# Hybrid encoder layer on Trainium2: the mixer's norm factors by power, attention heads in pairs, probabilities flipped by bank

## The chip, the cores and the metric

The kernel runs on one core of a Trainium2 chip. The metric is the device time of one execution in microseconds (us). Before the change it is 1005.02 us in the median of three runs (1003.6 to 1005.17). The engines are named as in the profile: PE (TensorE, matrix products; PEld its weight loads), DVE (VectorE), ACT (ScalarE), POOL (GpSimd) and SP (SyncE, which issues the loads). SBUF is the memory on the chip; PSUM is the small memory of eight banks into which PE writes, a bank holding 512 float32 numbers in each of 128 partitions.

## What is computed

One layer over 512 tokens of 1024 channels in float32, cut here to its frame:

```python
x = x + 0.5 * swiglu(rmsnorm(x, ffn1_norm), ffn1_w_gate, ffn1_w_up, ffn1_w_down)
proj = rmsnorm(x, mix_norm) @ w_in                     # 1024 -> 3*512 + 256 + 128 + 32
qa, ka = rmsnorm(q part by head, a_q_norm), rmsnorm(k part by head, a_k_norm)
out_a = chunked_relbias_attention(qa, ka, va, a_rel_bias)   # A: 8 heads of 64
out_b = mla_attention(...)                             # B: 8 heads, q and k of 64 + 32, v of 64
x = x + concat(out_a, out_b) @ w_out
x = x + 0.5 * swiglu(rmsnorm(x, ffn2_norm), ffn2_w_gate, ffn2_w_up, ffn2_w_down)
x = rmsnorm(x, final_norm)
```

`rmsnorm` multiplies by `rsqrt(mean(x*x) + EPS)` and a gain. Both attentions are softmax attentions in which a query sees its own chunk of 64 tokens and the chunks before it; A adds a bias by relative position to the scores, B makes q and k from low-rank latents and turns 32 of their columns by a rotary table. Every query and key part is normed (mean over 64, 32, 256 or 128 columns), which needs one factor per token and head.

## The kernel before

The work is staged as feed-forward block 1, mixer, feed-forward block 2. Every matrix product is split into a high and a low part so that three passes give float32 accuracy (`mm3`, lines 153 to 156): each product is three matmuls, on lines 154, 155 and 156. Weights come from HBM in units of 1024 columns (tag "raw", four buffers) and are split by ACT (high) and POOL or DVE (low) into tags "whi" and "wlo" (`wunit`, lines 140 to 151). The order on every engine is worked out by a scheduler when the kernel is built: it goes by the order of the program, shifted forward by 150 instructions where `tc.high_priority(offset=150)` stands, and by when a buffer of a tag comes free; a tile takes a free buffer of its tag when its first write is scheduled.

The mixer (lines 243 to 574) first makes the projections (`in_proj`, lines 310 to 320): the latents, qA, kA and vA, each as eight rank-128 steps into four banks, one for each 128 tokens. `bank` (lines 305 to 308) gives the banks: group 0 is s, s, tr, tr, group 1 is t, t, t, pv. The latents, uq, ukv and the value projection use group 1, qA and kA group 0. From the sums of squares `factors` (lines 272 to 285) makes the norm factors: a multiply and an add on DVE, then `rsqrt` (lines 116 to 123), which is Ln and Exp on ACT (each with a load of its table) and a refining step of four DVE instructions. POOL scales qB and kB and does the rotary turn (`rope`, lines 287 to 300).

Then the 16 heads run through a pipeline (lines 562 to 574), of three steps for each head:
- `front` (lines 464 to 501): PE transposes q and k into a "tr" bank, ACT and DVE copy the high and low part out (`evac`, lines 456 to 458). For A one transpose serves two heads, whose channels are partitions 0 to 63 and 64 to 127; the bias is loaded by SP, negated by DVE and masked by POOL.
- `softmax` (lines 503 to 523): for the query blocks i = 3, 2, 1, 0 PE makes the scores into "s" banks (512, 384, 256 and 256 columns, causal), DVE adds the bias and takes the minimum (line 518), ACT takes the exponential and its sum (line 520), DVE the reciprocal (line 521), POOL multiplies (line 522).
- `flip` and `values` (lines 525 to 559): PE transposes the probabilities, ten blocks of 128 x 128 in the order of the query blocks, into three "t" banks; ACT and DVE copy high and low parts into "whi" and "wlo" buffers; then PE multiplies with the values into the "pv" bank, two heads into one.

After it come `w_out` and the second feed-forward block, whose last norm uses POOL's power on 128 x 2 numbers (line 626).

Of the kernel before, what the change touches and what calls it, by code (L numbers as in the profile page):

```python
# [10 lines left out]
F32 = mybir.dt.float32  # L11
# [6 lines left out]
P = 128  # L18
# [6 lines left out]
NH = 8  # L25
# [14 lines left out]
def tile_macaron_block(  # L40
# [203 lines left out]
    with tc.tile_pool(name="mix", bufs=1, side="left", reuse_waits="tile") as mp:  # L244
# [24 lines left out]
        dve.tensor_scalar(out=nq[:, 0:1], in0=g(C_AQ), scalar1=-(HD ** -0.5), scalar2=None, op0=ALU.mult)  # L269
        dve.tensor_scalar(out=nq[:, 1:2], in0=g(C_BQ), scalar1=-(QK ** -0.5), scalar2=None, op0=ALU.mult)  # L270

        def factors(ss, n, width, scaled, name):

            f = mp.tile([P, NT, n], F32, tag="f_" + name, name="f_" + name)
            y = mp.tile([P, NT, n], F32, tag="y_" + name, name="y_" + name)
            y2 = mp.tile([P, NT, n], F32, tag="z_" + name, name="z_" + name)
            if scaled:
                dve.tensor_tensor(out=f, in0=ss, in1=vtok.unsqueeze(2).broadcast_to([P, NT, n]), op=ALU.mult)
                dve.tensor_scalar(out=f, in0=f, scalar1=1.0 / width, scalar2=EPS, op0=ALU.mult, op1=ALU.add)
            else:  # L280
                dve.tensor_scalar(out=f, in0=ss, scalar1=1.0 / width, scalar2=EPS, op0=ALU.mult, op1=ALU.add)
            rsqrt(f, f, y, y2)
            if scaled:
                dve.tensor_tensor(out=f, in0=f, in1=rtok.unsqueeze(2).broadcast_to([P, NT, n]), op=ALU.mult)
            return f
# [16 lines left out]
        with tc.tile_pool(name="ps2", bufs=1, space=PSUM, reuse_waits="tile") as ps:  # L302
            NB = {"s": 2, "tr": 2, "t": 3, "pv": 1}

            def bank(group, i, name):

                tag = (("s",) * NB["s"] + ("tr",) * NB["tr"], ("t",) * NB["t"] + ("pv",) * NB["pv"])[group][i]
                return ps.tile([P, 512], F32, tag=tag, name=name, bufs=NB[tag])
# [26 lines left out]
            yt = mp.tile([P, NT], F32, tag="yt", name="yt")  # L335
            zt = mp.tile([P, NT], F32, tag="zt", name="zt")
            rsqrt(rtok, vtok, yt, zt)
# [5 lines left out]
            fcq = factors(ssl[:, 0], 1, 256, True, "cq")  # L343
            fkv = factors(ssl[:, 1], 1, 128, True, "ckv")
            fkr = factors(ssl[:, 2], 1, 32, True, "kr")
# [17 lines left out]
            def qk_proj(off, dst, name):  # L363
# [4 lines left out]
                f = factors(ss, NH, HD, True, name)  # L368
# [26 lines left out]
            fn = factors(ssn, NH, HD, False, "qn")  # L395
            fp = factors(ssp, NH, ROPE, False, "qp")
# [27 lines left out]
            fk = factors(ssk, NH, HD, False, "kn")  # L424
# [37 lines left out]
            shared = {}  # L462

            def front(h):

                if h < NH:
                    if h % 2 == 0:
                        pr = h // 2
                        hs = slice(pr * P, (pr + 1) * P)
                        qh, ql, kh, kl = sets[0 if pr == 0 else 1 + (pr - 1) % 2]  # L470
                        evac(qh, ql, transposes(lambda t: qA[:, t, hs]), nq[:, 0:1])
                        evac(kh, kl, transposes(lambda t: kA[:, t, hs]), g(C_AK))
                        shared["A"] = qh, ql, kh, kl
                    r = slice((h % 2) * HD, (h % 2 + 1) * HD)
                    ops = tuple(t[r, :] for t in shared["A"])
                    bias = mp.tile([P, S], F32, tag="bias", name="bias", bufs=2)
                    nc.sync.dma_start(out=bias, in_=bias_tab[h])
                    dve.tensor_scalar(out=bias, in0=bias, scalar1=-1.0, scalar2=None, op0=ALU.mult)
                    pool.memset(bias[0:HD, S - HD:S], BIG)
                    return ops + (bias,)  # L480
                b = h - NH
                if b == 0:
# [8 lines left out]
                    pool.memset(mask[0:HD, S - HD:S], BIG)  # L491
# [9 lines left out]
                return qh[0:QK, :], ql[0:QK, :], kh, kl, mask  # L501

            def softmax(qh, ql, kh, kl, bias):

                pa = wraw.tile([P, 1024], F32, tag="raw", name="pa")
                pb = wraw.tile([P, 1024], F32, tag="raw", name="pb")
                pi = [pb[:, 256:384], pb[:, 0:256], pa[:, 512:896], pa[:, 0:512]]
                mn = small.tile([P, NT], F32, tag="mn", name="mn", bufs=4)
                sm = small.tile([P, NT], F32, tag="sm", name="sm", bufs=4)
                s3 = ps.tile([P, 512], F32, tag="s", name="s3", bufs=NB["s"])  # L510
                s2 = ps.tile([P, 512], F32, tag="s", name="s2", bufs=NB["s"])
                s01 = ps.tile([P, 512], F32, tag="s", name="s01", bufs=NB["s"])
                for i, so in ((3, s3), (2, s2), (1, s01[:, 256:512]), (0, s01[:, 0:256])):
# [11 lines left out]
            def flip(pi):  # L525
# [9 lines left out]
                for i in (3, 2, 1, 0):  # L535
                    for j in range(i + 1):
                        tt, o = where[j]
                        pe.transpose(tt[:, o + i * P:o + (i + 1) * P], pi[i][:, j * P:(j + 1) * P], ident)  # L538
# [189 lines left out]
```

## Time and profile before

| | before |
|---|---|
| median of 3 runs | 1005.02 us (1003.6 to 1005.17) |
| profiled execution | 1005.75 us, its span in the trace 1004.0 us |
| PE busy | 980.4 us (98%), 4579 matmuls |
| DVE, ACT, POOL busy | 397.7, 387.3, 591.5 us (40%, 39%, 59%) |
| chain that ended last | PE 88%, DVE 4%, POOL 2%, DMA 2%, ACT 1% |

The feed-forward blocks fill the first 390 and the last 410 us; the projections of the mixer lie at about 390 to 490 us and the heads at about 480 to 588 us, partly over one another. An engine's busy time counts a matmul to its modelled end, and matmuls overlap: so the distance from one start to the next, not the duration, tells what a matmul costs PE. In a timeline the idle time ahead of an instruction and what ended it stand in brackets. PEclk is the granted clock of PE, 1.00 being the higher of its two levels, 2.4 GHz, and 0.5 the lower, 1.2 GHz.

### The profile page before, as it was taken

Reading aid. Unit: us, or ns where it says so; the run is one execution under the profiler, and the core shown is the slowest. Engines: PE = TensorE matmul, PEld = TensorE weight load, DVE = VectorE, ACT = ScalarE, POOL = GpSimd, SP = SyncE. Lnnn points to the kernel's source line nnn. Section 1 sums busy time; section 2 is a strip of 40 time slices with the busy share of each in tenths; the row PEclk is TensorE's granted clock in tenths of the full one; section 3 lists DMA queues with packets and bytes.
Section 4 is the critical chain, followed back from the end, with each engine's and each line's share of the span. In section 5 each row is a group of like instructions: output and inputs, shape, how many; then the busy total and the mean of one; then the engine's idle time right before and its main releaser. Section 6 shows DMA issues by size and latency. Waiting matters only on the chain.

```text
span 1004.0 us, 12060 instructions
## 1 busy us (share of the span) xinstructions
PE 980.4 (98%) x4579; PEld 813.8 (81%) x4579; DVE 397.7 (40%) x687; ACT 387.3 (39%) x648; POOL 591.5 (59%) x429
## 2 busy tenths in 40 slices
PE   7999999999999999998999999999999999999996
PEld 4888888888888889786778988888888888888886
DVE  7533333432212215677688855243332333200002
ACT  4333233332222225754578853252332323322320
POOL 8586667667555522277345577677657666645540
PEclk8999999999999999999999999999999999999998
DMA  6422222232333334210010053223332322333302
GB/s 204 140 97 101 94 100 88 101 105 79 95 95 99 95 102 127 84 63 1 22 43 1 2 189 105 84 86 103 105 104 85 105 95 90 90 104 95 100 16 84
DMA packets 28714, 89.90 MB, mean 90 GB/s; under 512 B 3440, under 2 KB 5616, under 8 KB 28656
## 3 DMA queue, kind: packets, MB, share of 16 engines
q1 hardware_dynamic: 27504, 88.08, 27.4%
q10 hardware_dynamic: 1152, 1.05, 0.3%
q8 instruction: 36, 0.59, 0.2%
q14 instruction: 22, 0.18, 0.1%
HBM read 87.02 MB, written 2.10 MB: 89 GB/s over the span
## 4 chain that ended last, share of the span: by engine, by line
PE 88%; DVE 4%; POOL 2%; issue 2%; DMA 2%; ACT 1%; SPq 0%; POOLq 0%; DVEq 0%; ACTq 0%
PE gu L155 16%; PE gu L156 16%; PE gu L154 16%; PE dn L156 8%; PE dn L154 8%; PE dn L155 8%; PE pj L156 2%; PE pj L154 2%; PE pj L155 2%; PE wo L154 1%; PE wo L156 1%; PE wo L155 1%; PE t L538 1%; PE s L154 1%; PE tr L453 1%
## 5 line engine op out<-in xcount | busy, mean ns | idle before, releaser
L150 POOL TENSOR_TENSOR wlo<-raw,whi 128x1024 fp32r<-128x1024 f32 x138 | 323.5, 2345 | 152.0 <-ACT whi L149 152.0
L149 ACT CAST whi<-raw 128x1024 fp32r<-128x1024 f32 (+3 forms) x165 | 166.9, 1012 | 456.5 <-PE gu L155 258.0
L155 PE MATMUL gu<-xl,whi 128*128 128x512 f32 x352 | 139.4, 396 | 3.8 <-DVE xl L104 3.6
L154 PE MATMUL gu<-xh,whi 128*128 128x512 f32 x352 | 138.7, 394 | 0.8 <-ACT whi L149 0.8
L156 PE MATMUL gu<-xh,wlo 128*128 128x512 f32 x352 | 138.6, 394 | 0.0
L154 PE MATMUL gu<-x2h,whi 128*128 128x512 f32 x352 | 136.9, 389 | 0.0
L155 PE MATMUL gu<-x2l,whi 128*128 128x512 f32 x352 | 136.8, 389 | 0.0
L156 PE MATMUL gu<-x2h,wlo 128*128 128x512 f32 x352 | 136.8, 389 | 0.0
L169 POOL TENSOR_TENSOR us<-us,gs 128x512 f32<-128x512 f32 x44 | 58.1, 1321 | 108.6 <-DVE us L167 106.8
L168 DVE SCALAR_TENSOR_TENSOR gs<-th,gs 128x512 f32<-128x512 f32 x44 | 90.9, 2069 | 31.8 <-ACT th L166 31.8
L165 DVE TENSOR_TENSOR gs<-gu,rs 128x512 f32<-128x512 f32 x44 | 30.4, 691 | 175.3 <-PE gu L156 163.3
L202 DVE SCALAR_TENSOR_TENSOR x<-dn,x 128x512 f32<-128x512 f32 (+1 forms) x17 | 11.2, 660 | 193.7 <-PE dn L156 193.7
L155 PEld LDWEIGHTS gu<-xl,whi 128*128 128x128 f32 x352 | 66.9, 190 | 21.2 <-DVE xl L104 7.8
L154 PEld LDWEIGHTS gu<-xh,whi 128*128 128x128 f32 x352 | 67.2, 191 | 15.6 <-ACT whi L149 1.6
L156 PEld LDWEIGHTS gu<-xh,wlo 128*128 128x128 f32 x352 | 66.9, 190 | 13.9 <-DVE wlo L150 0.2
L155 PEld LDWEIGHTS gu<-x2l,whi 128*128 128x128 f32 x352 | 66.1, 188 | 13.8
L156 PEld LDWEIGHTS gu<-x2h,wlo 128*128 128x128 f32 x352 | 66.1, 188 | 13.8
L154 PEld LDWEIGHTS gu<-x2h,whi 128*128 128x128 f32 x352 | 66.1, 188 | 13.6
L154 PE MATMUL dn<-h1h,whi 128*128 128x512 f32 x176 | 68.5, 389 | 0.0
L155 PE MATMUL dn<-h1l,whi 128*128 128x512 f32 x176 | 68.5, 389 | 0.0
L156 PE MATMUL dn<-h1h,wlo 128*128 128x512 f32 x176 | 68.5, 389 | 0.0
L167 DVE SCALAR_TENSOR_TENSOR us<-gu,rs 128x512 f32<-128x512 f32 x44 | 30.3, 689 | 65.2 <-PE gu L156 65.2
(318 smaller groups left out, 1826.8 us busy)
## 6 DMA issues: line engine op xcount, KB each, us to landing
raw<-in_gu SPq DMA_DIRECT2D x87, 512.0 KB, 3.6
raw<-in_dn SPq DMA_DIRECT2D x32, 512.0 KB, 3.5
raw<-in_dn SPq DMA_DIRECT2D x16, 384.0 KB, 3.1
raw<-in_w_in SPq DMA_DIRECT2D x12, 512.0 KB, 3.4
raw<-in_w_out SPq DMA_DIRECT2D x8, 512.0 KB, 4.4
x<-in_xT SPq DMA_DIRECT2D x8, 256.0 KB, 5.5
bias<-in_bias_tab SPq DMA_DIRECT2D x8, 256.0 KB, 2.8
raw<-in_w_in SPq DMA_DIRECT2D x4, 416.0 KB, 3.3
```

The costliest lines, as they stand in the source:

```text
L149: act.copy(hi[:, cc], raw[:, cc])
L150: (lo_on or pool).tensor_tensor(out=lo[:, cc], in0=raw[:, cc], in1=hi[:, cc].bitcast(F32), op=ALU.subtract)
L154: pe.matmul(out, lhsT=ah, rhs=bh, start=start, stop=False)
L155: pe.matmul(out, lhsT=ah, rhs=bl, start=False, stop=False)
L156: pe.matmul(out, lhsT=al, rhs=bh, start=False, stop=stop)
L165: dve.tensor_tensor(out=gs, in0=gup[0], in1=rs, op=ALU.mult)
L167: dve.scalar_tensor_tensor(out=us, in0=gup[1], scalar=0.5, in1=rs, op0=ALU.mult, op1=ALU.mult)
L168: dve.scalar_tensor_tensor(out=gs, in0=th, scalar=1.0, in1=gs, op0=ALU.add, op1=ALU.mult)
L169: pool.tensor_tensor(out=us, in0=us, in1=gs, op=ALU.mult)
L202: dve.scalar_tensor_tensor(out=x[dt][:, h], in0=pt[:, h], scalar=0.5, in1=x[dt][:, h], op0=ALU.mult, op1=ALU.add)
L453: pe.transpose(pt[0:src(t).shape[1], t * P:(t + 1) * P], src(t), ident)
L538: pe.transpose(tt[:, o + i * P:o + (i + 1) * P], pi[i][:, j * P:(j + 1) * P], ident)
```

## The change

Four things are changed, all in the mixer.
- `factors` and `rtok` use one POOL instruction that raises to the power -0.5, in place of Ln, Exp and the refining step; several norms go through one call (the three of the latents; the two of qB).
- The banks: "s" has four (was two), "tr" one (was two), "t" two (was three). Group 0 is s four times, group 1 is t, t, tr, pv.
- A's heads go through `front` and `softmax` in pairs. For each query block the score matmuls of the two heads are issued in turn, each head on its half of the rows. The bias is no longer negated: the queries keep their sign and the DVE instruction scales by -1. The second head's bias sits in the tag "wc"; the probabilities of i = 1 sit in halves of `rs` and `ssum`, the others in one "raw" buffer instead of two.
- One reciprocal over all four query blocks of a head, after its last exponential, and then POOL's four products. `flip` goes bank by bank (keys 3 and 2, keys 1, keys 0), each copied out as soon as it is full.

```diff
-        def factors(ss, n, width, scaled, name):
...
+        mhalf = mp.tile([P, 2 * NT * NH], F32, tag="mhalf", name="mhalf")
+        pool.memset(mhalf, -0.5)
+        def factors(parts, n, scaled, name):
+            f = mp.tile([P, len(parts), NT, n], F32, tag="f_" + name, name="f_" + name)
+            for i, (ss, width) in enumerate(parts):
...
+                dve.tensor_scalar(out=f[:, i], in0=src, scalar1=1.0 / width, scalar2=EPS, op0=ALU.mult, op1=ALU.add)
+            flat = f.rearrange("p i t n -> p (i t n)")
+            pool.tensor_tensor(out=flat, in0=flat, in1=mhalf[:, 0:len(parts) * NT * n], op=ALU.pow)
...
-            NB = {"s": 2, "tr": 2, "t": 3, "pv": 1}
+            NB = {"s": 4, "tr": 1, "t": 2, "pv": 1}
...
-                tag = (("s",) * NB["s"] + ("tr",) * NB["tr"], ("t",) * NB["t"] + ("pv",) * NB["pv"])[group][i]
+                tag = (("s",) * 4, ("t", "t", "tr", "pv"))[group][i]
...
-            rsqrt(rtok, vtok, yt, zt)
+            pool.tensor_tensor(out=rtok, in0=vtok, in1=mhalf[:, 0:NT], op=ALU.pow)
...
-            fcq = factors(ssl[:, 0], 1, 256, True, "cq")
-            fkv = factors(ssl[:, 1], 1, 128, True, "ckv")
-            fkr = factors(ssl[:, 2], 1, 32, True, "kr")
+            fcq, fkv, fkr = factors([(ssl[:, 0], 256), (ssl[:, 1], 128), (ssl[:, 2], 32)], 1, True, "lat")
...
+            def front_a(pr):
...
+                evac(qh, ql, transposes(lambda t: qA[:, t, hs]), nq[:, 0:1])
+                evac(kh, kl, transposes(lambda t: kA[:, t, hs]), g(C_AK))
+                for e in range(2):
+                    bias = (mp.tile([P, S], F32, tag="bias", name="bias", bufs=2) if e == 0
+                            else work.tile([P, S], F32, tag="wc", name="bias"))
+                    nc.sync.dma_start(out=bias, in_=bias_tab[2 * pr + e])
+                    pool.memset(bias[0:HD, S - HD:S], -BIG)
...
+            def softmax(heads):
...
+                for i in (3, 2, 1, 0):
...
+                        bk = [ps.tile([P, 512], F32, tag="s", name=f"s{i}", bufs=NB["s"]) for _ in heads]
...
+                    for j, (a, b) in enumerate(((0, 2), (0, 3), (1, 2))):
+                        for o, hd in zip(so, heads):
+                            pe.matmul(o, lhsT=hd[a][:, ii], rhs=hd[b][:, 0:nn], start=j == 0, stop=j == 2)
+                    for o, hd, (pi, mn, sm) in zip(so, heads, out):
+                        dve.tensor_tensor_reduce(out=pi[i], in0=o[:, 0:n], in1=hd[4][:, S - n:S], op0=ALU.add, op1=ALU.min,
+                                                 scale=-1.0, scalar=3e38, accum_out=mn[:, i:i + 1])
+                        act.activation(pi[i], pi[i], AF.Exp, bias=mn[:, i:i + 1], scale=-1.0, accum_out=sm[:, i:i + 1])
+                for pi, mn, sm in out:
+                    dve.reciprocal(sm, sm)
+                    for i in (3, 2, 1, 0):
+                        pool.tensor_tensor(out=pi[i], in0=pi[i], in1=sm[:, i:i + 1].broadcast_to([P, (i + 1) * P]), op=ALU.mult)
...
+                for keys, copies in ((((3, 0), (2, -256)), (...)), (((1, -128),), (...)), (((0, 0),), (...))):
+                    tt = ps.tile([P, 512], F32, tag="t", name="tp", bufs=NB["t"])
+                    for j, o in keys:
+                        for i in range(NT - 1, j - 1, -1):
+                            pe.transpose(tt[:, o + i * P:o + (i + 1) * P], pi[i][:, j * P:(j + 1) * P], ident)
+                    for h_, l_, c0, c1 in copies:
+                        act.copy(h_, tt[:, c0:c1])
+                        dve.tensor_tensor(out=l_, in0=tt[:, c0:c1], in1=h_.bitcast(F32), op=ALU.subtract)
...
+            fronts = [lambda pr=pr: front_a(pr) for pr in range(4)] + [lambda b=b: front_b(b) for b in range(NH)]
...
             for it in range(-2, n + 1):
+                pis = prob.pop(it, [None])
+                for e, pi in enumerate(pis):
...
+                        cur = head, flip(pi)
...
+                    if e == 0:
+                        with (tc.high_priority(offset=150) if it < 1 else ExitStack()):
+                            if 0 <= it + 1 < n:
+                                prob[it + 1] = softmax(qk.pop(it + 1))
+                            if it + 2 < n:
+                                qk[it + 2] = fronts[it + 2]()
+                    if last:
+                        values(*last)
+                    last = cur
```

## Rows read from the trace of the kernel before

**Rows 1.** windows: stretch, length, busy of PE, PEld, DVE, ACT, POOL; PEclk, DMA, GB/s

```profile
469.90:474.13 4.23, 0.00 (x1) 0.03 (x1) 2.98 (x9) 1.03 (x2) 0.51 (x3) 1.00 0.00 0
474.13:490.00 15.87, 15.87 (x71) 12.25 (x71) 6.72 (x16) 6.13 (x14) 1.87 (x2) 0.89 0.00 0
490.00:580.00 90.00, 88.60 (x573) 74.31 (x573) 77.93 (x277) 71.78 (x209) 48.29 (x97) 1.00 0.07 19
541.00:588.50 47.50, 46.82 (x318) 42.22 (x317) 39.38 (x137) 40.02 (x111) 26.10 (x47) 1.00 0.13 45
```

**Rows 2.** timeline of PE: start, us, line, out<-in, shapes, count [idle before]

```profile
474.13 1.09 PE L453 MATMUL tr<-ident,qA 128*128 128x128 f32 x4 [4.25 <-DVE kA L371]
...
477.56 0.39 PE L154 MATMUL pj<-whi,xh 128*128 128x512 f32 x1
477.79 0.39 PE L155 MATMUL pj<-wlo,xh 128*128 128x512 f32 x1
...
489.98 0.50 PE L156 MATMUL pj<-whi,xl 128*128 128x512 f32 x1
...
498.26 0.48 PE L154 MATMUL pv<-PAh,VAh 128*128 128x512 f32 x1
```

**Rows 3.** timeline of PE where two heads' scores meet (x2: merged)

```profile
501.62 0.28 PE L156 MATMUL pv<-PBh,VAl 128*128 128x256 f32 x1
501.83 0.49 PE L154 MATMUL s<-xh,xh 64*128 64x512 f32 x2
...
502.72 0.33 PE L538 MATMUL t<-ident,pb 128*128 128x128 f32 x1
```

**Rows 4.** timeline of PE, end of one head's scores

```profile
504.51 0.28 PE L155 MATMUL s<-xl,xh 64*128 64x256 f32 x1
504.62 0.28 PE L156 MATMUL s<-xh,xl 64*128 64x256 f32 x1
504.83 0.33 PE L538 MATMUL t<-ident,pb 128*128 128x128 f32 x1
```

**Rows 5.** timeline of DVE, the factors of kA

```profile
470.98 0.19 DVE L120 TENSOR_TENSOR z_ka<-y_ka 128x32 f32<-128x32 f32 x1 [1.83 <-ACT y_ka L119]
...
472.10 2.48 DVE L371 TENSOR_TENSOR kA<-pj,f_ka 128x512 f32<-128x512 f32 x4
```

**Rows 6.** waits of PE from 395 to 600: us in total, times, longest

```profile
PE pj L154 <- DVE qA L371: 1.2, 1, 1.2
```

**Rows 7.** line 626, the power at the kernel's end: min/median/max ns

```profile
L626 POOL TENSOR_TENSOR rc<-rc,mhalf x2: 693/700/708, 988.7 to 995.7; 128x2 f32<-128x2 f32 x2
```

**Rows 8.** timeline of POOL from the scaling of qB on

```profile
442.85 5.04 POOL L399 TENSOR_TENSOR qB<-qB,f_qn 128x512 f32<-128x512 f32 x4 [0.19 <-DVE f_qp L123]
...
470.20 0.21 POOL L540 MEMSET PBh<- 128x128 f32 x1
```

**Rows 9.** groups of DVE from 474 to 588: count | busy us, mean ns

```profile
L521 DVE RECIPROCAL sm<-sm 128x1 f32<-128x1 f32 x64 | 9.0, 151 | 1.3 <-ACT pb L520 0.6 <-ACT pa L520 0.5
...
L478 DVE TENSOR_SCALAR bias<-bias 128x512 f32<-128x512 f32 x6 | 3.5, 579 | 0.7 <-DMA bias<-in_bias_tab 0.7
```

**Rows 10.** groups of ACT from 474 to 588, the exponentials

```profile
L520 ACT ACTIVATE pa<-pa,mn 128x512 f32<-128x512 f32 (+1 forms) x32 | 21.6, 674 | 2.3 <-DVE mn L518 2.0
...
L520 ACT ACTIVATE pb<-pb,mn 128x256 f32<-128x256 f32 (+1 forms) x32 | 14.5, 454 | 0.1
```

**Rows 11.** groups of POOL, 474 to 588, the products with the reciprocals

```profile
L522 POOL TENSOR_TENSOR pa<-pa,sm 128x512 f32<-128x512 f32 (+1 forms) x32 | 29.8, 932 | 38.3 <-DVE sm L521 37.6 <-PE t L538 0.2
L522 POOL TENSOR_TENSOR pb<-pb,sm 128x256 f32<-128x256 f32 (+1 forms) x32 | 16.3, 511 | 13.8 <-DVE sm L521 13.8
```

**Rows 12.** timelines of PE, ACT, DVE: a head of B in "tr"

```profile
556.30 0.60 PE L453 MATMUL tr<-ident,kB 128*64 128x128 f32 x4
...
559.24 0.67 ACT L457 ACTIVATE kst<-tr,col 64x512 fp32r<-64x512 f32 x1
...
559.61 0.74 DVE L458 SCALAR_TENSOR_TENSOR ql<-tr,nq,qh 96x512 fp32r<-96x512 f32 x1
```

More of the change, by code (lines that the diff above doesn't have):

```diff
@@ L268, in tile_macaron_block @@
         nq = mp.tile([P, 2], F32, tag="nq", name="nq")
[L269 to L285 removed]
+        dve.tensor_scalar(out=nq[:, 0:1], in0=g(C_AQ), scalar1=HD ** -0.5, scalar2=None, op0=ALU.mult)
@@ L461, in tile_macaron_block, with front_b @@
                     (XH[4], XL[4], XH[5], XL[5]), (XH[6], XL[6], XH[7], XL[7])]
[L462 to L481, printed above, removed]
+            shared = {"n": 0}
+            def front_a(pr):
+                hs = slice(pr * P, (pr + 1) * P)
+                qh, ql, kh, kl = sets[0 if pr == 0 else 1 + (pr - 1) % 2]
+                evac(qh, ql, transposes(lambda t: qA[:, t, hs]), nq[:, 0:1])
+                evac(kh, kl, transposes(lambda t: kA[:, t, hs]), g(C_AK))
+                out = []
+                for e in range(2):
[3 more added lines that the diff above has]
+                    pool.memset(bias[0:HD, S - HD:S], -BIG)
+                    r = slice(e * HD, (e + 1) * HD)
+                    out.append((qh[r, :], ql[r, :], kh[r, :], kl[r, :], bias))
+                return out
+            def front_b(b):
                 if b == 0:
@@ L490, in front @@
                     pool.memset(mask, 0.0)
[L491 removed]
+                    pool.memset(mask[0:HD, S - HD:S], -BIG)
                     shared["B"] = kst, mask
@@ L500, in front @@
                 evac(kh[0:HD, :], kl[0:HD, :], kp[0:HD, :], g(C_BK, rows=HD))
[L501 to L513, printed above, removed]
+                return [(qh[0:QK, :], ql[0:QK, :], kh, kl, mask)]
+            def softmax(heads):
+                out = []
+                for _ in heads:
+                    pa = wraw.tile([P, 1024], F32, tag="raw", name="pa")
+                    c = 256 * (shared["n"] % 2)
+                    pb = (rs, ssum)[shared["n"] // 2 % 2][:, c:c + 256]
+                    shared["n"] += 1
+                    pi = [pa[:, 896:1024], pb, pa[:, 512:896], pa[:, 0:512]]
+                    mn = small.tile([P, NT], F32, tag="mn", name="mn", bufs=4)
+                    sm = small.tile([P, NT], F32, tag="sm", name="sm", bufs=4)
+                    out.append((pi, mn, sm))
+                s01 = None
+                for i in (3, 2, 1, 0):
                     n = (i + 1) * P
```

59 lines of the change are left out of this document (23 added, 36 removed).

## The prediction

> **What bounds the kernel now.** I read the page first: TensorE (PE) is busy for nearly the whole span in both feed-forward blocks, which the change leaves alone, so the mixer alone is in question. Then I cut the mixer's second half into stretches [rows 1]: PE does nothing for 4.2 us from 469.9 on, runs at a mean granted clock of 0.89 until 490 (after that stop the lower of its two levels, 1.2 GHz, for 2 x 0.11 x 15.87 = 3.5 us, then 2.4), and is then busy 88.6 of 90 us, with VectorE (DVE) at 77.9, ScalarE (ACT) at 71.8 and GpSimd (POOL) at 48.3. PE is the bound there; DVE is a close second. The timeline of PE [rows 2] shows why it stopped: the transposes of `front` hold for kA (4.25 us), because their PSUM tag "tr" is part of the key projection's bank group. The matmuls of the value projection (`pj`) come after it, the last at 489.98. They fill PE while the first heads go through their softmax; the first value matmul (`pv`) is at 498.26. Start to start a 512-column matmul takes 0.23 us (477.56 to 477.79), a 256-column one 0.12 (504.51 to 504.62 [rows 4]), so a 384-column one is put at 0.174.
>
> **The sum, against the profiled execution of 1005.75 us** (0.7 above the median of the runs shown; the forecast is moved by as much).
>
> Scores of A. One head costs 3 x (0.227 + 0.174 + 2 x 0.117) = 1.9 us of PE, eight heads 15.2. The two heads of a pair stand in row halves 0-63 and 64-127. That such matmuls overlap is already seen: at 501.83 two 64-row matmuls start together and both series of three are gone by 502.72 [rows 3], in the time of the 512-column series. There are five such meetings in the trace; each hides 3 x 0.117 = 0.35 us, 1.75 in all. The change pairs all: -7.6 + 1.75 = -5.85 us, as far as PE is the bound.
>
> Switches. Going from 128 rows to 64 costs 0.09 us over the normal step (501.62 to 501.83 is 0.21, normal 0.12 [rows 3]), coming back as much (504.62 to 504.83 [rows 4]). I count 25 visits to 64-row work (481.98 the first, 535.74 the last); four per pair make 16. Nine less at 0.18: -1.6 us.
>
> The wait for kA. The factors of kA go through ACT's Ln and Exp and four DVE steps; DVE waits 1.83 us for ACT at 470.98 and kA is written from 472.10 [rows 5]. With one power on POOL this is shorter, and, more to the point, "tr" leaves that bank group: PE goes on with `pj`. The stop (4.2) and the slow clock behind it (3.5 us at half, 1.7) go: -5.9 us. The wait of `pj` for qA (1.2 [rows 6]) goes likewise: -1.2.
>
> The power itself. The trace has it only with 2 columns: 0.70 us [rows 7]. The change asks for 4, 12, 32, 64, 32 and 32. Lower bound: nothing grows, 0.7 each. Upper bound: all of the time over a plain 0.2 us (a small clear on POOL [rows 8]) is per column, 0.25 us a column, so 16 us for 64 columns. I take the lower end with some growth (about 1.5 us for 64), because the short call is likely to be mostly fixed cost; both ends are kept. It waits in POOL's in-order queue for DVE's scaled sums; behind it stand the squares, the rotary steps and the scalings of qB and kB (442.85 to 470.4, almost without a gap [rows 8]). DVE's product with rtok and the weights' low parts behind it wait for POOL as they wait for ACT now. With the small price kA is ready near 469, long before it is needed (below), so nothing is added. The factors of the latents, and rtok, come earlier too; PE is in qA's projection then and waits for none of them, so that is worth 0.
>
> What the banks take away. The value projection now sits in t, t, tr, pv, and "tr" is one bank. So the key transposes of pair 0 wait for the end of the value projection and its copies, and behind them in PE's queue stand all scores: PE's filler is used up before attention begins. Packed, `pj` ends near 479. From there to the first value matmul: copies out of "tr" 1.4 (0.67 + 0.74 [rows 12]), transposes 0.5, copies 1.4, first scores 0.7, min on DVE 0.6, seven of eight exponentials of the pair 4.0 (per head 2 x 0.674 + 2 x 0.454 = 2.26 [rows 10]), reciprocal 0.15, POOL's four products 2.9 (2 x 0.932 + 2 x 0.511 [rows 11]), flip and copy 0.8, with about 1 us of handovers: 13.5 us. PE has 8.5 us of work in it (transposes of three pairs 2.2, scores of two pairs 5.2, a flip 1.1), so 5.0 idle; if the clock falls once, 1.7 more: +6.7 us. (The exponential's table, until now loaded by the factors, is loaded here, in ACT's wait for the first scores: 0; without that cover it would cost less than the 1.83 us that DVE now waits for a load and an exponential.)
>
> One bank less for "tr" and for "t". In B each head transposes q and k into "tr"; before, the k transposes at 556.30 did not wait for q's copies, which ended at 560.35 [rows 12]. With one bank they must. If PE always finds other work this costs 0; if never, the 1.4 us of copies a head, 11 us. The B stretch has PE at 46.8 of 47.5 us [rows 1], so work is at hand: I take 0.3 a head, +2.4. Flipping bank by bank holds a "t" bank for a shorter time, so two of them are put at no cost, PE's scores and value products standing between (without these a copy pair, 1.1 us a head); four "s" banks at a small gain, below.
>
> One reciprocal a head. 48 x 0.151 = 7.2 us of DVE go, and 6 x 0.579 = 3.5 with the negation of the biases (two were made earlier) [rows 9]; DVE is not the bound, and only its short waits before scores go: -0.9. But POOL's products of a head now start after its last exponential; for the last head nothing hides that: between 0 and 2.4 us (2.9 less the one 0.5 step that follows now), taken +1.5. The bias loads are the same eight, two to a front; on SP's queue only the w_out loads stand behind them, due 40 us later. pb in rs and ssum frees staging buffers, for which nothing on PE waits now: 0.
>
> Sum: -5.85 - 1.6 - 5.9 - 1.2 + 6.7 + 2.4 + 1.5 - 0.9 = -4.85 us: 1005.02 - 4.85 = 1000.2 us.
>
> **The rivals.** (a) POOL's power is paid by the column: 0.25 us x 128 columns (qB's 64, kB's 32, kA's 32) = 32 us on a queue that has some 11 us to spare (ready at 469, needed at 480). It decides from 0.09 us a column; at the full price kA comes near 495 to 499 and PE stands still for some 15 us: 1015, slower. For it: 2 columns already take 0.70 us. Against it: nothing is known of 64.
> (b) The single "tr" bank starves B: 1.4 us x 8 instead of 2.4: 1009, slower. For it: k's copy on ACT starts 3 us after its transposes [rows 12]; against it: PE's other work.
> (c) The copies bind. In 490 to 580 PE's 88.6 falls by 8.35 to some 80, ACT's 71.8 does not fall, DVE's 77.9 falls to 67. ACT would have to be at 0.88 of such a stretch, DVE's share now; if it can't pass its present 0.80, the stretch stays at 90 and the 8.35 us come back: 1003.6, no change. The Trainium skill (TensorEngine Tiling (Array Packing), "PSUM Bottleneck") says this in general: tiling makes TensorE faster but not the emptying of PSUM. By it the sum would be that of this rival, by the rows DVE ran at 0.87 for 90 us, so I do not follow it.
> (d) The scheduler lets pair 0's key transposes into "tr" ahead of the value projection; then `pj` still fills the start: 6.7 less, 993.5.
> (e) The change does not do what it says: the two heads' score matmuls are not issued in turn, and nothing overlaps: 1006, slower by a hair.
>
> **How the numbers follow.** Forecast 0.48, (a) 0.10, (b) 0.13, (c) 0.15, (d) 0.09, (e) 0.05. A change under 0.2% (2 us) can't be told from none by a measurement of this kernel. Of the forecast's own range (997 to 1003.5) 0.45 is faster and 0.03 the same; with (d) and a little of (c) faster is 0.57, the same 0.18, slower 0.25. The range runs to (b) and (d) and leaves the far end of (a) out: 992 to 1010.
>
> **What would show it.** Right: no wait of PE for kA; score matmuls of A starting two by two, 48 pairs; `pj` packed up to about 479 and then a thin stretch of some 13 us before the first value matmul; B as dense as now. Wrong: powers over 3 us each and PE waiting for kA; PE waiting for the copies out of "tr" in B; ACT without gaps from 490 on while PE waits; a first value matmul after 498.26, where it is now [rows 2].

## The result: 25 us slower, and the profile after

| | before | after |
|---|---|---|
| median, same chip | 1005.1 us (4 runs, 1003.6 to 1006.12) | 1030.24 us (4 runs, 1029.38 to 1032.41) |
| ratio, 95% interval | | 1.0255 [1.0234, 1.0276] |
| span of the profiled execution, mean granted clock | 1004.0 us, 0.991 | 1028.9 us, 0.979 |
| first `pj` to first score of A | 105.7 us | 116.7 us |
| A's first score to B's first | 53.0 us | 43.5 us |
| B's first score to the first matmul of `wo` | 53.2 us | 77.1 us |

The last three lines are read from the timelines of PE, from start to start, and add up to the stretch from the latents' first `pj` to the first `wo` (211.9 and 237.3 us); outside it the two executions agree within 0.5 us. So the loss has two places: 10.9 us ahead of attention and 23.9 us from B's first score on; A itself is 9.4 us shorter. The windows of after, columns as in [rows 1]:

```profile
460.00:480.00 20.00, 17.87 (x79) 14.45 (x77) 5.16 (x9) 1.90 (x4) 20.00 (x12) 1.00 0.00 0
480.00:500.00 20.00, 8.49 (x38) 5.92 (x39) 8.94 (x27) 7.52 (x20) 5.88 (x6) 0.52 0.00 0
500.00:520.00 20.00, 17.78 (x99) 12.98 (x97) 12.73 (x41) 13.00 (x39) 11.83 (x24) 0.72 0.15 53
...
560.00:580.00 20.00, 16.61 (x110) 13.83 (x109) 13.28 (x41) 13.38 (x39) 8.11 (x16) 1.00 0.00 1
580.00:600.00 20.00, 16.94 (x109) 14.52 (x110) 13.38 (x40) 12.71 (x37) 9.44 (x20) 1.00 0.08 28
600.00:620.00 20.00, 16.98 (x95) 13.95 (x95) 6.42 (x12) 9.84 (x17) 10.24 (x11) 1.00 0.48 155
```

POOL is busy without a gap from 460 to 480. PE works 8.49 us of the next 20, and its clock falls to the lower level and is back only after 500. In B (its last score ends at 592.96, `wo` starts at 613.34) PE has 16.6 to 17.0 of 20 us where it had 46.8 of 47.5 [rows 1]; DVE and ACT are no fuller than before, so no other engine took over as the bound. The waits of PE from 360 to 620 (total, times, longest), where before the waits for kA (4.25 us [rows 2]) and for qA [rows 6] were the longest:

```profile
PE tr L452 <- DVE VAl L444: 10.2, 1, 10.2
PE tr L452 <- DVE ql L457: 7.7, 8, 1.0
PE s L524 <- DVE mn L526: 2.6, 10, 0.5
PE pv L154 <- ACT PAh L552: 2.3, 3, 1.5
PE tp L550 <- DVE PAl L553: 1.9, 5, 0.9
```

**The start.** Timeline of after, on POOL, DVE and PE:

```profile
441.85 10.55 POOL L285 TENSOR_TENSOR f_qb<-f_qb,mhalf 128x64 f32<-128x64 f32 x1 [0.20 <-DVE f_qb L283]
...
462.40 5.42 POOL L285 TENSOR_TENSOR f_ka<-f_ka,mhalf 128x32 f32<-128x32 f32 x1
...
470.58 5.42 POOL L285 TENSOR_TENSOR f_kn<-f_kn,mhalf 128x32 f32<-128x32 f32 x1
...
483.75 1.25 POOL L304 TENSOR_TENSOR qB<-rtmp 128x512 f32<-128x512 f32 x1
485.06 0.95 POOL L436 MEMSET VAl<- 128x1024 f32 x1
...
485.04 3.23 DVE L444 SCALAR_TENSOR_TENSOR VAl<-pj,rtok,VAh 128x256 fp32r<-128x256 f32 x8 [14.47 <-POOL qB L304]
...
477.48 0.39 PE L156 MATMUL pj<-whi,xl 128*128 128x512 f32 x1
488.02 1.08 PE L452 MATMUL tr<-ident,qA 128*128 128x128 f32 x4 [10.15 <-DVE VAl L444]
...
492.68 0.79 PE L524 MATMUL s<-qk,qk 64*128 64x512 f32 x2 [0.84 <-ACT qk L456]
```

Three powers of 64, 32 and 32 columns take 21.4 us of POOL. Behind them in its queue the rotary step ends at 485.0; before, all of this was over by 470.2 [rows 8]. VAl lies in the buffer (tag "vAl") that the rotary step uses as scratch. So DVE cannot copy the values out before 485.04, the value projection's four banks stay taken, "tr" among them, and the transposes that open attention wait 10.15 us.

**The heads of B.** One head on PE, ACT and DVE:

```profile
551.51 0.92 PE L524 MATMUL s<-kst,qh 96*128 96x512 f32 x4
...
553.10 0.60 PE L452 MATMUL tr<-ident,qB 128*96 128x128 f32 x4
...
553.73 0.69 ACT L456 ACTIVATE qh<-tr,nq 96x512 fp32r<-96x512 f32 x1 [1.44 <-PE tr L452]
...
554.17 0.42 DVE L526 CUSTOM_DVE_ANT_0 ssum<-s,mask 128x256 f32<-128x256 f32 x1 [1.15 <-PE tp L550]
...
554.52 0.69 DVE L526 CUSTOM_DVE_ANT_0 pa<-s,mask 128x512 f32<-128x512 f32 x1
...
555.61 0.74 DVE L457 SCALAR_TENSOR_TENSOR ql<-tr,nq,qh 96x512 fp32r<-96x512 f32 x1
...
556.50 0.60 PE L452 MATMUL tr<-ident,kB 128*64 128x128 f32 x4 [0.98 <-DVE ql L457]
...
557.13 0.68 ACT L456 ACTIVATE kst<-tr,col 64x512 fp32r<-64x512 f32 x1 [0.28 <-PE tr L452]
557.85 0.74 DVE L457 SCALAR_TENSOR_TENSOR kst<-tr,col,kst 64x512 fp32r<-64x512 f32 x1 [0.50 <-ACT kst L456]
...
559.16 0.92 PE L524 MATMUL s<-kst,qh 96*128 96x512 f32 x4
```

This is a closed loop over the one "tr" bank: scores, q into the bank, its copy on ACT, its low part on DVE (queued behind the reductions of the scores just made), k into the bank, flips and values on PE beside k's two copies, the next scores. One turn takes 559.16 - 551.51 = 7.65 us, and the seven turns of B take 7.5 to 7.7; before, they took 4.0 to 7.5, in the mean 5.5. PE's waits show 1.2 us of a turn (0.98 at k's transposes and 0.20 at the last scores). The last leg is not set by k's copies: they end at 558.59, and PE comes to the next scores only at 559.16, after the values.

The "tr" bank is not all that closes the loop. The reductions, behind which q's low part stands, themselves wait in every turn for PE's flips, which stand behind q's transposes. DVE's waits from B's first score to its last:

```profile
DVE rs L526 <- PE tp L550: 7.0, 4, 2.4
DVE ssum L526 <- PE tp L550: 6.4, 4, 2.2
```

`rs` and `ssum` hold the probabilities of i = 1 for four heads. So the scores run four heads ahead of the flips and then wait until the flips of the head four before have read its buffer. How much of a turn is due to the one bank and how much to these buffers, no run separates; that the bank has a large part is shown below (e4, e5).

**Behind the last score.** Only 11.4 of the 23.9 us lie between B's first score and the end of its last (45.4 us before, 56.7 after). The other 12.5 us come behind it: 7.9 us to `wo` before, 20.4 after. PE in after:

```profile
592.67 0.28 PE L524 MATMUL s<-kst,ql 96*128 96x256 f32 x1
592.79 0.40 PE L154 MATMUL pv<-PAh,VBh 128*128 128x512 f32 x1
...
597.82 0.47 PE L154 MATMUL pv<-PAh,VBh 128*128 128x512 f32 x1 [0.73 <-DVE xl L568]
...
601.68 0.49 PE L154 MATMUL pv<-PAh,VBh 128*128 128x512 f32 x1 [0.35 <-ACT PAh L552]
...
606.15 0.47 PE L154 MATMUL pv<-PAh,VBh 128*128 128x512 f32 x1 [0.73 <-DVE xl L568]
...
610.80 0.50 PE L154 MATMUL pv<-PAh,VBh 128*128 128x512 f32 x1 [1.46 <-ACT PAh L552]
...
613.34 0.39 PE L154 MATMUL wo<-xh,whi 128*128 128x512 f32 x1
```

The values of five heads are still to be done (60 of the 192 value matmuls; before the change it was 30), and PE takes them one after another, 2.5 to 5.0 us each, waiting for copies in between. Two of them were put off in A: at B's first score the values of four heads were done; before the change it was six. So part of A's 9.4 us is no gain. By an estimate from the start-to-start distances of before (a head's value matmuls 1.9 us, its ten transposes of 0.11 us 1.1) two heads make 6 us.

### The profile page after: what moved, and what is told of

Same layout as the page of the kernel before. It is cut to its first block, busy times and chain, and to the rows that moved or that the text cites. A ratio compares the mean times of both kernels' runs of the same rounds, so it can differ in the third digit from the quotient of the medians.

```text
span 1028.9 us, 11948 instructions
## 1 busy us (share of the span) xinstructions
PE 981.2 (95%) x4579; PEld 812.7 (79%) x4579; DVE 381.1 (37%) x595; ACT 367.1 (36%) x616; POOL 614.2 (60%) x436
## 5 line engine op out<-in xcount | busy, mean ns | idle before, releaser
L167 DVE SCALAR_TENSOR_TENSOR us<-gu,rs 128x512 f32<-128x512 f32 x44 | 30.4, 690 | 65.2 <-PE gu L156 65.2
```

The source lines that it names most:

```text
L167: dve.scalar_tensor_tensor(out=us, in0=gup[1], scalar=0.5, in1=rs, op0=ALU.mult, op1=ALU.mult)
```

## The experiments

The table has all runs, medians beside before on the same chip; the last columns are the three stretches of the first table, from each profiled execution, which may lie some us off its median (e3's took 1021.54, e4's 1016.59). In e4, e5, e8 and e20 the number of "s" banks changes along with the bank under test, and so do the groups of the projections.

| run | us | before | ratio, 95% | to A | A | B to wo |
|---|---|---|---|---|---|---|
| e1_ln_exp_factors | 1023.66 | 1005.03 | 1.0190 [1.0175, 1.0205] | 108.9 | 44.5 | 77.1 |
| e3_tr_free_of_values | 1016.34 | 1005.03 | 1.0108 [1.0091, 1.0125] | 103.6 | 48.5 | 77.0 |
| e13_ln_exp_and_tr_free | 1023.84 | 1005.03 | 1.0192 [1.0169, 1.0216] | 111.5 | 41.0 | 77.1 |
| e5_two_tr_three_s | 1012.96 | 1005.03 | 1.0074 [1.0048, 1.0099] | 102.7 | 46.6 | 71.0 |
| e2_power_only | 1005.35 | 1004.24 | 1.0010 [1.0001, 1.0020] | 102.7 | 53.4 | 55.2 |
| e4_one_tr | 1019.09 | 1004.24 | 1.0150 [1.0118, 1.0182] | 110.2 | 46.8 | 67.2 |
| e6_all_but_banks | 1007.46 | 1004.24 | 1.0039 [1.0023, 1.0054] | 102.7 | 51.8 | 60.9 |
| e7_flips_by_bank | 1004.08 | 1004.24 | 0.9994 [0.9984, 1.0003] | 107.0 | 50.0 | 56.4 |
| e8_two_t_banks | 1014.58 | 1004.61 | 1.0097 [1.0082, 1.0112] | 108.9 | 50.2 | 61.8 |
| e9_one_reciprocal | 1018.14 | 1004.61 | 1.0138 [1.0121, 1.0155] | 105.7 | 59.1 | 62.8 |
| e12_pairs_only | 1002.85 | 1004.61 | 0.9981 [0.9971, 0.9990] | 104.7 | 49.9 | 54.0 |
| e11_pairs_over_s_and_tr | 997.33 | 1004.61 | 0.9923 [0.9906, 0.9939] | 104.2 | 44.0 | 56.5 |
| e17_reciprocal_and_flips | 1019.88 | 1004.27 | 1.0148 [1.0132, 1.0165] | 105.8 | 56.8 | 65.2 |
| e18_reciprocal_a_block | 1029.27 | 1004.27 | 1.0248 [1.0231, 1.0265] | 118.2 | 41.9 | 76.5 |
| e14_best_reciprocal_a_block | 997.52 | 1004.27 | 0.9930 [0.9916, 0.9945] | 104.2 | 43.1 | 57.6 |
| e16_best_ln_exp | 998.81 | 1004.27 | 0.9942 [0.9927, 0.9957] | 105.3 | 44.2 | 55.3 |
| e19_reciprocal_four_buffers | 1012.59 | 1004.03 | 1.0085 [1.0070, 1.0100] | 105.6 | 57.8 | 56.2 |
| e20_three_t_one_tr | 1022.44 | 1004.03 | 1.0181 [1.0164, 1.0198] | 103.5 | 47.7 | 78.6 |

### The start: power or banks

```diff
 # e1 (on after; rtok likewise)
-            pool.tensor_tensor(out=flat, in0=flat, in1=mhalf[:, 0:len(parts) * NT * n], op=ALU.pow)
+            rsqrt(flat, flat, y, y2)
 # e3 (on after)
-                tag = (("s",) * 4, ("t", "t", "tr", "pv"))[group][i]
+                tag = (("s", "s", "s", "tr"), ("s", "t", "t", "pv"))[group][i]
 # e13: both.   e5 (on after)
+            NB = {"s": 3, "tr": 2, "t": 2, "pv": 1}
+                tag = (("s", "s", "tr", "tr"), ("s", "t", "t", "pv"))[group][i]
```

> The changed kernel with only the power taken back: every norm factor and rtok by Ln and Exp and four DVE operations, in the new joined tiles; pairs, banks, reciprocal and flips as changed. Power theory: the 21.4 us of powers on POOL between 441.85 and 476 (10.55 + 5.42 + 5.42) put the end of the rope chain, behind which VAl's memset and DVE's copies of the values stand, at 485, and TensorE's 10.2 us stop before the first transpose out of the bank that the copies hold follows from it. Then without the powers the rope chain is over before the value projection ends (477.5), the stop shrinks to the time of the copies, 3 to 4 us, and some of the slow clock behind it (granted 0.52 in 480 to 500) goes: 1030 - 7 - 4 = 1019, between 1013 and 1024. Bank theory (the power is immaterial; what costs is that the transposes' only bank belongs to the value projection, so that nothing of attention can run beside it): the stop stays near 10 us and the time within 3 us of the changed kernel, 1027 to 1031.

Measured 6.6 us less than after, as the power theory had it. VAl is cleared at 467.7 and PE's stop ahead of the transposes is 1.8 us:

```profile
477.94 0.39 PE L156 MATMUL pj<-whi,xl 128*128 128x512 f32 x1
480.13 0.63 PE L453 MATMUL tr<-ident,qA 128*128 128x128 f32 x4 [1.80 <-DVE VAl L445]
```

> The changed kernel with the power kept, but with the eight banks grouped otherwise: q and k projections take three s banks and the tr bank, the value projection one s bank, both t banks and pv. So the transposes of the first pair wait for kA alone (ready at 470.6) and not for the values' copies. Bank theory: transposes and first scores run beside the value projection, the 10.2 us stop goes and with it most of the slow clock: 1030 - 10 - 5 = 1015, between 1011 and 1020. Power theory in its strict form (POOL's late end holds the start whatever the banks are, since the first flips need a t bank that the values' copies hold until 488 and the first values need VAl): the stop moves from the transposes to the flips, and less than half is won, 1022 to 1028. B theory (most of the 25 us lies in the heads of B, about 1 us a head at the one tr bank and more behind it): under 5 us won, 1025 or more.

Measured 13.9 less than after, the bank theory's range, with the power in place. The profiled execution, at 1021.54, shows 8.2 of it in the three stretches; its mean granted clock was 0.984, that of the other four 0.991 to 0.994. The transposes slip in between `pj` and the scores follow `pj` at once:

```profile
472.99 0.39 PE L156 MATMUL pj<-whi,xl 128*128 128x512 f32 x1
473.22 0.60 PE L452 MATMUL tr<-ident,qA 128*128 128x128 f32 x4
473.57 0.48 PE L154 MATMUL pj<-whi,xh 128*128 128x512 f32 x1
...
477.09 0.60 PE L452 MATMUL tr<-ident,kA 128*128 128x128 f32 x4
478.47 1.70 PE L524 MATMUL s<-qk,qk 64*128 64x512 f32 x8 [0.78 <-ACT qk L456]
```

> Both of the former together: Ln and Exp for the factors, and the tr bank outside the value projection's group. If power and banks together are the whole start of attention, what is left against the kernel before is the one tr bank in B (7.7 us of waits in 8 heads in the changed kernel's trace, against 0 before) less what the paired scores save (5.85 by the prediction): 1005 + 8 - 6 = 1007, between 1003 and 1012. If something else in the new order (reciprocal at the end of a head, flips bank by bank over two banks) costs as much, it stays over 1012.

A miss: 1023.84, 7.5 above e3. With "tr" out of the way the power is by the medians the better of the two, and the traces have a reason: kA is written by 469.2 in e3, by 474.2 in e13, where PE again stops 5.1 us for it. The profiled executions themselves (1021.54 and 1021.67) don't show the difference, so its place is argued and not shown; the other executions of e13 had a mean granted clock of 0.981 to 0.985, where those of e3 had 0.991 to 0.994. Against e1, freeing "tr" brings nothing without the power (1023.66 and 1023.84): the 13.9 us of e3 hold for the kernel with the power alone. What is shown is that the powers cost where something that PE needs stands behind them (6.6 us, e1).

> The changed kernel with the power kept and the banks three s, two tr, two t, one pv; the value projection takes s, t, t, pv. Start of attention as with tr free of values, and B's transposes have two banks as before. B theory: the waits of B's transposes for the copies (7.7 us in 8) go, and the time is 7 us under that of the kernel that only frees tr; with the start's gain, near 1008, between 1004 and 1014. Against it: B's waits are only passed on to the next late thing (the scores' three banks, the flips' two), and the time is within 2 us of the kernel that only frees tr. Three s banks for pairs may cost in A up to 4 us.

3.4 under e3, half of what was expected. B's stretch is 6.0 shorter: its turns fall to 5.4 to 8.1 us, in the mean 6.2, so the second "tr" bank shortens the loop, but five heads' values stay behind the last score, with 21.7 us to `wo`. Both readings were partly right.

### One edit at a time on the kernel before

```diff
 # e2: factors and rtok by pool.tensor_tensor(..., op=ALU.pow), nothing else
 # e4
-            NB = {"s": 2, "tr": 2, "t": 3, "pv": 1}
+            NB = {"s": 3, "tr": 1, "t": 3, "pv": 1}
 # e7: flip() of the changed kernel.   e8: e7 and
+            NB = {"s": 3, "tr": 2, "t": 2, "pv": 1}
+                tag = (("s", "s", "tr", "tr"), ("s", "t", "t", "pv"))[group][i]
 # e9 (behind the loop over i); e17: e7 and e9
+                dve.reciprocal(sm, sm)
+                for i in (3, 2, 1, 0):
+                    pool.tensor_tensor(out=pi[i], in0=pi[i], ...)
 # e19: e9 and
+                pb = (rs, ssum)[shared["n"] // 2 % 2][:, c:c + 256]
+                pi = [pa[:, 896:1024], pb, pa[:, 512:896], pa[:, 0:512]]
 # e12 (on after): factors, banks, reciprocals and flips of before;
 #   pairs, bias without negation and buffers as changed
```

> The kernel before with only the norm factors and rtok by POOL's power (seven powers, of 4, 4, 4, 4, 32, 32, 32, 32 and 32 columns); banks, heads, reciprocal and flips as before. Freeing the tr bank gave more with the power than with Ln and Exp (1016.3 against 1023.8), so the power itself is taken to bring kA forward: kA's last write came at 470.6 in the changed kernel against 474.6 before, and TensorE's stops of 4.25 us for kA and 1.2 us for qA go: 1005 - 4.5 = 1000.5, between 998 and 1004. Power theory in its strict form (POOL busy until 485 with powers and rope holds VAl's memset, the values' copies and the first heads' normalising): the copies of the values, at 488 to 495 before, come later by 3 to 5 us: 1006 to 1010.

Neither: no difference beyond 0.2%. The windows of e2 show why:

```profile
460.00:480.00 20.00, 20.00 (x94) 16.11 (x93) 6.30 (x10) 3.33 (x7) 20.00 (x13) 1.00 0.00 0
480.00:500.00 20.00, 16.05 (x81) 11.48 (x79) 16.23 (x55) 13.10 (x36) 13.88 (x21) 0.83 0.10 27
```

The stop for kA is gone (20.00), but `pj` now ends at 478.1 and not at 490, so nothing fills PE beside the first heads' softmax (16.05, clock 0.83). The 4 us are given back one stretch later.

> The kernel before with one tr bank and three s banks in place of two and two; q and k projections take three s and tr, the value projection t, t, t and pv as before. Nothing else. B theory: a head of B loses about 1 us at the one bank, as in the changed kernel (7.7 us in 8 waits of at most 1.0), and A's pairs lose as often at their eight transposes: 1005 + 9 = 1014, between 1009 and 1018. The prediction's term for the one bank, 0.3 us a head: 1005 + 2.4 = 1007.5, between 1005 and 1009. No cost at all (the scores' third bank pays for it): 1004 to 1006.

14.9 slower (its four runs lie between 1016.5 and 1023.2), 1 us above B theory's range. B to `wo` takes 67.2 instead of 53.2, all of it in the turns (6.9 to 10.3 us); behind the last score it is 7.5 us, as before.

> The kernel before with only the order of the flips changed: bank by bank, each bank's copies behind its own transposes, over three t banks. If the flips' order is neutral while there are three banks: 1003.5 to 1006.5. If it is this order, not the two banks, that stretches the end of attention (in the changed kernel TensorE's heads of the last stretch come 5.1, 3.9, 4.4 and 4.7 us apart, before 3.6, 4.8 and 2.2): 4 to 8 us more, 1009 to 1013.

Neutral, as expected.

> The kernel before with the flips bank by bank (alone 1004.1, the same as before) over two t banks and not three; the bank set free is a third s bank, the value projection takes s, t, t, pv, and tr keeps two. If two t banks make the tail (from the end of the last scores to the first matmul of wo 20.5 us in the changed kernel and in all three of its variants with one tr, 21.7 with two tr, 11.7 with three t banks and all other edits, 8.0 before): 1005 + 9 = 1014, between 1009 and 1018. If the tail comes from the heads of B that run late for other reasons, and two t banks cost only their own waits (1.9 us in 5 in the changed kernel): 1004 to 1008.

10.0 slower, in the first range. But the tail from which that range came is 11.6 us here and not 20: of the 8.6 us that B to `wo` is longer, 3.7 lie in it and 4.9 ahead of it. So the number came out by luck in part: two "t" banks by themselves leave hardly more values behind the last score (2.9 heads, before 2.5).

> The kernel before with only one reciprocal a head, behind the fourth block, and the four normalisations after it. What the changed kernel with the banks of before costs over the kernel before is 3.2 us, of which the power is 1.1 and the flips -0.2; left are 2.3 for pairs and reciprocal together. If the late reciprocal is what costs (probabilities of the first block come one head's reductions later, so flips and values come later at the start and at the end): 1006 to 1009. If it is neutral and saves DVE its 48 short operations beside TensorE: 1003 to 1005.5, and the loss is in the pairs.

13.5 slower, over the range of the "late" theory. The windows of e9 around the first heads:

```profile
496.00:500.00 4.00, 2.02 (x13) 1.54 (x13) 1.46 (x6) 1.32 (x5) 4.00 (x7) 1.00 0.21 66
500.00:504.00 4.00, 3.50 (x11) 2.19 (x12) 2.66 (x9) 2.64 (x8) 0.83 (x5) 0.64 0.00 0
504.00:508.00 4.00, 4.00 (x18) 3.81 (x16) 1.36 (x4) 1.57 (x4) 0.41 (x2) 0.50 0.00 0
```

The first heads' products come at once (POOL 4.00 of 4 from 496 to 500) while PE does 2.02 us of work, and the clock halves behind it. A takes 59.1 instead of 53.0, B to `wo` 62.8 instead of 53.2.

> The kernel before with one reciprocal a head (alone 1018.1) and flips bank by bank (alone 1004.1) together; all else as before. If the late reciprocal costs because the flips row by row hold all three t banks while they wait for the last block: with flips by bank it costs little, 1004 to 1009. If it costs because everything of a head comes later (normalising, flips, and with them the buffers of two heads back), whatever the flips' order: 1016 to 1020.

15.6 slower, in the second range: the order of the flips is not what makes the late reciprocal dear.

> The kernel before with one reciprocal a head (alone 1018.1) and with pb in rs and ssum, so that a head takes one raw buffer of the four and not two. If the late reciprocal costs because two heads' buffers are all there are, and a later normalising holds back the reductions of the head after next: 1004 to 1009. If it costs by itself: 1016 to 1020.

Between the two: 8.6. Two heads' buffers were part of the loss (B to `wo` is 56.2, not 62.8); A stays at 57.8. What holds A there is not settled.

> The kernel before with A's heads in pairs, their score matmuls in turn in the two row halves, biases added without DVE's negation; factors by Ln and Exp, a reciprocal a block, flips row by row over three banks, two s and two tr banks as before. The prediction's term: -5.85 for the scores, -1.6 for the switches: 997.6, between 995 and 1001. If the shorter scores only let TensorE wait for DVE, ACT and POOL (A's span from its first score to B's first was 53.7 before and 51.7 in the changed kernel with these banks): 1003 to 1007. If two s banks for two heads cost more than the pairing brings: 1007 to 1011.

1.8 less, 0.15 under the range of "PE only waits". In its trace 20 of A's 48 pairs of score matmuls start within 0.07 us of each other; in after 40 do, in before 10.

### All but the banks, and a version faster than both

```diff
 # e6 (on after): NB and bank() of before
 # e11: e6 and
-                        bk = [ps.tile([P, 512], F32, tag="s", ...) for _ in heads]
+                        bk = [ps.tile([P, 512], F32, tag=tg, ...) for _ in heads
+                              for tg in ["tr" if i == 2 and len(heads) == 2 else "s"]]
 # e14: e11 with a reciprocal a block.   e16: e14 with Ln and Exp
 # e18: after with a reciprocal a block.   e20 (on after)
+            NB = {"s": 3, "tr": 1, "t": 3, "pv": 1}
+                tag = (("s", "s", "s", "tr"), ("t", "t", "t", "pv"))[group][i]
```

> The changed kernel with all its edits but the banks: two s, two tr, three t and one pv, the value projection on the three t banks and pv, as in the kernel before. Bank theory (the banks alone make the change slow; power, pairs, one reciprocal and flips bank by bank are worth what they were meant to be): 1005 - 4.5 for kA - up to 5.9 for the paired scores = 996, between 993 and 1003. Against it, two s banks for the two heads of a pair: each of four blocks waits for the reductions of the block before, about 1.5 us more a block in three of four blocks of four pairs, of which half is hidden: 1005 - 4.5 - 5.9 + 9 = 1003.6. And if the reciprocal at the end of a head and the flips bank by bank lengthen the tail (20 us from the last score to wo in the changed kernel, 8 before) by themselves: 1008 or more.

3.2 over before, 22.8 under after: nine tenths of the loss hang on the banks. The time lies between the second reading (1003.6) and the third (1008 or more), and both have a part: with two s banks for two heads A keeps 51.8 us, and behind the last score it is 11.7 us to `wo` instead of 7.9.

> A version meant to be faster: all edits with the banks of before (that was 1007.5), and A's pairs put their second block's scores into the two tr banks, which A's transposes need only twice a pair, so that a block no longer waits for the reductions of the block just before it. If the two s banks limit A: its span falls from 51.7 to about 45 and the time to 1007.5 - 5 = 1002, between 998 and 1004. If A is limited by its copies, reductions and exponentials in any case, or the transposes now wait for the scores' reductions: 1006 to 1010.

997.33, 7.3 under before and just under the range: A falls to 44.0. Its timeline has two 512-column matmuls in the 0.23 us of one, and its windows show PE full from 500 to 560 (from 480 to 500 it has 16.65 us, at a clock of 0.83):

```profile
508.31 0.57 PE L524 MATMUL s<-xl,xh 64*128 64x512 f32 x2
508.54 0.56 PE L524 MATMUL s<-xh,xl 64*128 64x512 f32 x2
```

```profile
500.00:520.00 20.00, 20.00 (x133) 16.41 (x132) 15.78 (x53) 17.35 (x51) 10.35 (x25) 1.00 0.01 2
520.00:540.00 20.00, 19.80 (x138) 18.15 (x136) 16.02 (x45) 15.11 (x40) 9.49 (x20) 1.00 0.01 1
540.00:560.00 20.00, 20.00 (x142) 18.35 (x142) 18.08 (x55) 17.49 (x53) 11.97 (x22) 1.00 0.00 1
```

> The changed kernel with a reciprocal a block and the normalising behind each block, as before; the power, pairs, banks and flips as changed. If the late reciprocal costs in the changed kernel what it cost alone: 1030 - 11 = 1019, between 1015 and 1022. If the heads of B run in the loop over the one tr bank (7.6 us a head, every head alike) and the late reciprocal is hidden behind it: 1026 to 1031. DVE has 48 more short operations between the reductions and the copies that the loop waits for: up to 3 us a longer loop, 1031 to 1034.

1.0 less: in the changed kernel the late reciprocal is hidden.

> The fastest version so far (997.3; all edits, the banks of before, A's second block over the tr banks) with a reciprocal a block. Late reciprocal costs there too: 990 to 995. Neutral with flips by bank: 996 to 999. DVE's extra operations cost: 999 to 1003.

0.2 more than e11: neutral there too.

> The same with a reciprocal a block and with the factors by Ln and Exp in place of the power. The power was neutral alone (+1.1) since the 4.25 us stop for kA that it took away came back as thin work between 480 and 500; if so here: within 2 us of the version with the power and a reciprocal a block. If the power's earlier kA is worth its 4 us where the banks let the scores start: 3 to 5 us more. If POOL's late end holds the first heads: 2 to 4 us less.

1.3 more than e14: power and Ln with Exp are worth the same within 2 us where the banks are right.

> The changed kernel with three t banks, three s, one tr, one pv: the value projection on t, t, t, pv, the tr bank free of it (with two t banks and four s that was 1016.3). If the two t banks cost in the changed kernel what they cost alone (10.0): 1008, between 1006 and 1011. If the loop over the one tr bank (7.6 us a head) sets B's pace whatever the t banks: 1013 to 1018.

A miss, outside both ranges: 6.1 above e3, not 8 below. The third "t" bank does its part at the end: two heads' values are left behind the last score and not five, and `wo` follows after 12.4 us and not 20.4. But B's turns grow to 7.9 to 9.8 us (7.5 to 7.7 in e3), and B to `wo` comes to 78.6. Why the turns grow (a fourth s bank gone is the other difference) stays open.

## Why the prediction was wrong, step by step

By the traces the loss divides into +10.9 us ahead of A, -9.4 in A, +11.4 in B's turns and +12.5 behind the last score. For the same places the sum had about -0.4 (-5.9 - 1.2 + 6.7), -7.45 (scores and switches), +2.4 and +1.5. Two of the signs named for being wrong came: PE waits for the copies out of "tr" in B, 7.7 us in all, and the first value matmul is at 514.99.

- *Scores of A* (-5.85) and *switches* (-1.6): the mechanism held, 40 of 48 pairs overlap in after, and the visits to 64-row work fall from 25 to 13 (16 were counted on). A is 9.4 us shorter, of which about 6 are values put off to the end, so that it comes near the forecast is luck. The pairing pays only with banks for both heads: -1.8 alone (e12), -5.5 with the second block in "tr" and the flips bank by bank as well (e16).
- *The wait for kA* (-5.9) and for qA (-1.2): both waits went. The gain did not: alone they came to +1.1 (e2), since the same `pj` that waited is the cover of the first heads. The step counted a stop as time won without asking what came late next.
- *The power*: priced at about 1.5 us for 64 columns; it took 10.55. I had both ends and chose the wrong one, from a single 2-column row [rows 7]. Rival (a) had the mechanism at 0.25 a column, measured 0.16, over the 0.09 from which it was to decide; but the place was wrong. kA was ready at 470.6; what came late was the rotary step, and behind it VAl. That the rotary steps stand behind the power on POOL was in the text [rows 8]; that VAl's buffer hangs on them was not.
- *Start of attention without `pj`* (+6.7): the right place, mis-sized. With the power the banks there cost 13.9 (e3); 6.6 go as well if the powers go (e1), and then the banks there cost nothing (e13). The sum took the copies of the values as done 1.4 us after `pj`; PE's transposes came 10.5 us after it.
- *One "tr" bank in B* (+2.4): the step that failed in its mechanism. By itself, with a third "s" bank, it costs 14.9 (e4), above the bound of 11. I asked how long PE would wait for a copy, and had PE's other work hide most of it. But the copies sit in a loop with the scores and the flips, whose turn is 7.65 us; PE's own waits show 1.2 of it. Rival (b), 1009 with 0.13, had the place, but at 1.4 us a head, the time of the copies alone.
- *Two "t" banks* (0): 10.0 by themselves, with a third "s" bank (e8). In the changed kernel they leave the values of five heads behind the last score, also with a reciprocal a block (e18): 20.4 us to `wo`, with three "t" banks 12.4 and two heads (e20). With two "tr" banks it is 21.7 and 11.7, and the time falls by 5.5 (e5 to e6); with one it does not fall, as the turns grow (e20). That these values would be late was not in the sum.
- *One reciprocal* (-0.9 and +1.5): 13.5 alone (e9). In the changed kernel it costs 1.0 (e18), in the fastest version nothing (e14). In the kernel before, the four heads' buffers that I had put at 0 take away a third of the loss (e19); the rest stays open.
- *Flips bank by bank*, alone: 0, measured -0.2 (e7).
- Rival (c), copies as the bound: DVE and ACT are at 13.3 of 20 us in B, not higher than before. The Trainium skill (TensorEngine Tiling (Array Packing), "PSUM Bottleneck") says that tiling speeds up TensorE but not the emptying of PSUM, which may then become the limit. The trace does not bear this out for the copying engines, with 13.3 of 20 us; what decided was the number of banks and how soon they came free.
- The parts do not add: 14.9 + 10.0 + 13.5 is 38.4, the whole change 25.1. The late reciprocal is hidden in after (e18), and the pairing takes some of the sum back; how the rest overlaps is not shown.

## What to carry to other kernels

Where a resource is cut from two to one, look for the loop that closes through it (produce, copy out on each engine with what is queued there, consume, produce again) and compare its length with the work of one turn; the wait seen on the busiest engine says little. Count also what is left to do when a stretch ends: a stretch that got shorter may have put its work off. Before a bank group is regrouped, list for each bank who holds it last and what that holder waits for. A price known from one small size is a price for that size.

## What the runs showed of the hardware

POOL's power goes by the column, at 128 partitions: 0.70 us for 2 columns [rows 7], and in after

```profile
L285 POOL TENSOR_TENSOR f_lat<-f_lat,mhalf x1: 2272/2272/2272, 399.7 to 399.7; 128x12 f32<-128x12 f32 x1
L285 POOL TENSOR_TENSOR f_qa<-f_qa,mhalf x1: 5442/5442/5442, 422.1 to 422.1; 128x32 f32<-128x32 f32 x1
L285 POOL TENSOR_TENSOR f_qb<-f_qb,mhalf x1: 10552/10552/10552, 441.8 to 441.8; 128x64 f32<-128x64 f32 x1
```

(durations in ns): (10552 - 2272) / 52 = 159 ns a column and about 0.4 us besides. And a thin start costs twice: after PE's 10.15 us stop the granted clock is 0.52 over 480 to 500 and 0.72 over 500 to 520, that is at the lower level for 0.96 and 0.56 of these stretches.
